# A one-core transformer block: large GpSimd operations moved to VectorE, ScalarE and TensorE

## The chip, the cores and the metric

The kernel runs as one program on one core of a Trainium2 chip. The metric is the time of one execution on the device, in microseconds (us). A core has five engines with queues of their own: TensorE (PE in the profile, its weight loads PEld), VectorE (DVE), ScalarE (ACT), GpSimd (POOL) and SyncE (SP), which here issues all transfers to 16 DMA engines.

## The reference

One block on 256 tokens of width 1024. All arithmetic is in float32.

```
mod = silu(c) @ ada_w + ada_b          # six vectors of 1024: sh1, sc1, g1, sh2, sc2, g2
h = rmsnorm(x) * (1 + sc1) + sh1
p_r, p_d, p_m = split(h @ w_in)
y_r = rwkv7_mix(p_r, ...)              # 4 heads, a recurrence over the tokens
y_d = diff_attention(p_d, ...)         # 4 heads, each the difference of two softmaxes
y_m = moba_attention(p_m, ...)         # 4 heads; one block of 256, so plain causal attention
x = x + g1 * (concat([y_r, y_d, y_m]) @ w_out)
h2 = rmsnorm(x) * (1 + sc2) + sh2
x = x + g2 * hier_moe(h2, ...)         # 32 experts, 2 of them for each token
```

## The kernel before

The program has a front and an expert stage. The front computes everything up to the sum with `g1 * mix`; the expert stage streams the weights of all 32 experts (192 MB, in 192 loads of 1 MB or their halves and quarters) through a ring of 20 buffers of 1 MB: `ringB` (10), `ringA` (2) and `ringC` (8). Most of these buffers serve the front first. The first four of `ringB` hold the RWKV part of `w_in`; the other six hold the recurrence's and the attention's tables. `ringA` holds the other pieces of `w_in` and two of the four pieces of `w_out`. `ringC` lies where the pools of the front lie. `wtile` (line 1152 on) gives buffers to the expert loads in the order ringB, ringA, ringC. A load can be issued once the tile that lay in its buffer is no longer read, and SP issues the loads one after the other.

In the front three pieces of work run interleaved. `rwkv` (the lead) is a chain of small steps. `attention` walks over 6 pairs of heads in eight steps: transposes of queries and keys (`heads_T`), logits and exponentials (`soft`), the weights (`weights`), their transposes (`probs_T`) and the products with the values. The fill work is pulled in between by `pull`, so many microseconds at a time: `proj_DM` multiplies `h` by the five pieces of `w_in` for the two attentions, in three products per step on a high part and a rest, which `split` makes (ACT copies the high part, line 313; line 314 subtracts it: on DVE for the first 16 of 40 steps, on POOL for the rest). Within `mixed`, after each unit of `proj_DM` 0.4 of a unit of the modulation follows: `columns` (sh2 and sc2, in dot products on DVE, line 364) and `gate` for g1 and g2. `gate` (line 437) multiplies 8 rows of `ada_w` by a column of silu(c) and sums them, in 16 DVE operations of 128x512 per gate, and then sums over the partitions with a matrix of ones on PE. The loads for these take turns in the two buffers of `ringF`. Loads of the front are tied to one order on SP by `load_next`.

`load_wo` (line 899) loads `w_out` in four pieces of 1 MB and multiplies each in place by g1, on POOL, in 16 operations of 128x512 (line 904). Pieces 1 and 2 lie in `ringA`, 0 and 3 in `ringF`. `proj_out` (line 907) then multiplies the mixed heads `mT` by it, in three sets: pieces 1 and 2 (diff attention), piece 0 (RWKV), piece 3 (MoBA), each as soon as its heads are done, and adds each result from PSUM to `x2` on DVE (line 925).

In `rwkv` ACT computes two sigmoids (line 535), two exponentials (lines 545 and 546) and, through `lam_of` (line 776), the exponentials of lambda. An activation function that isn't in the loaded table needs an ACT_TABLE_LOAD first. In `weights` (line 799) POOL scales one of the two exponentials (lines 805 and 808).

The order of instructions on each engine is fixed when the program is built, by a scheduler which lets a later instruction go first where an earlier one isn't ready by its own estimate; `behind` and `keep_in_program_order` tie pairs together. At run time each engine goes through its queue in that order.

Of the kernel before, what the change touches and what calls it, by code (L numbers as in the profile page):

```python
# [8 lines left out]
FT = mybir.dt.float32  # L9
# [85 lines left out]
def build(tc, ctx, a):  # L95
# [211 lines left out]
    def split(it):  # L307

        for x, (s_, k, w) in enumerate(it):
            if x == 2:  # L310
                wp[1] = fr.tile([128, 2, 2, 512], FR, name="wp1", tag="hT")
            hi, lo = (wp[x // 2 % 2][:, x % 2, q, :w.shape[-1]] for q in range(2))
            A.copy(hi, w)  # L313
            (V if x < 16 else G).tensor_sub(lo, w, hi)  # L314
            yield s_, k, hi, lo
# [104 lines left out]
    for dst_, n in ((g1b, 2), (g2b, 5)):  # L420
        G.memset(dst_, 0.0)
        load_next(dst_[0:1, :], a["ada_b"][0:1, 1024 * n:1024 * n + 1024])
# [13 lines left out]

    def gate(dst):

        for kc in range(4):
            w = take()  # L440
            for kk_ in range(2):
                for h in range(2):
                    f, k = slice(512 * h, 512 * h + 512), 2 * kc + kk_
                    V.scalar_tensor_tensor(dst[:, f], w[:, 1024 * kk_ + 512 * h:1024 * kk_ + 512 * h + 512],
                                           cs[:, k:k + 1], dst[:, f], op0=OP.mult, op1=OP.add)
            yield 0.2
        for h in range(2):
            f = slice(512 * h, 512 * h + 512)
            p = bank("bc")
            T.matmul(p, ones, dst[:, f], start=True, stop=True)  # L450
            A.copy(dst[:, f], p)
            yield 0.9
# [62 lines left out]
    def rwkv():  # L515
# [17 lines left out]
        for x, (z, b) in ((sw, (zw, "w0")), (ar, (za, "a0"))):  # L533
            for j in range(2):
                A.activation(x[:, j, :], z[:, S * j:S * j + S], AF.Sigmoid, bias=c_(b)[:, j:j + 1])
# [9 lines left out]
        A.activation(P[:, :, 1:65], c8(sw), AF.Exp, scale=lam0)  # L545
        A.activation(Pi, c8(sw), AF.Exp, scale=-lam0)
# [223 lines left out]
    def lam_of():  # L770
        lm = at.tile([128, 2, 64], FT, name="lm", tag="osq", bufs=1)
        lv = c_("lam").rearrange("p (a d) -> p a d", d=64)
        V.tensor_mul(lm, lv[:, 0::2, :], lv[:, 1::2, :])
        ls = small.tile([128, 4], FT, name="ls", bufs=1)
        V.tensor_reduce(ls[:, 0:2], lm, AX.X, OP.add)
        A.activation(ls[:, 2:4], ls[:, 0:2], AF.Exp)
        V.tensor_sub(nlam, ls[:, 3:4], ls[:, 2:3])
        V.tensor_scalar(nlam, nlam, -lam_init, None, op0=OP.add)
# [20 lines left out]
    def weights(i, e, ms, nk):  # L799
# [3 lines left out]
        if i < 4:  # L803
            V.tensor_mul(ms[:, 1:2], ms[:, 1:2], nlam)
            G.tensor_scalar(e[:, 1, :nk], e[:, 1, :nk], ms[:, 1:2], None, op0=OP.mult)
            V.scalar_tensor_tensor(w[0][:, r], e[:, 0, :nk], ms[:, 0:1], e[:, 1, :nk], op0=OP.mult, op1=OP.add)
        else:
            G.tensor_scalar(w[0][:, r], e[:, 0, :nk], ms[:, 0:1], None, op0=OP.mult)
# [90 lines left out]
    def load_wo(jj):  # L899
        w = ftile("rwo", ringF if jj in (0, 3) else ringA)  # L900
        load_next(w.rearrange("p (j n) -> p j n", j=2), wo[:, 2 * jj:2 * jj + 2, :])
        for q in range(4):
            f = slice(512 * (q % 2), 512 * (q % 2) + 512)
            G.tensor_mul(w[:, 512 * q:512 * q + 512], w[:, 512 * q:512 * q + 512], g1b[:, f])
        return w

    def proj_out():

        ws = {jj: load_wo(jj) for jj in (1, 2, 0, 3)}
        load_pk("C", const)  # L910
        for set_ in ((1, 2), (0,), (3,)):
            for j in set_:
                while ("j", 2 * j) not in done or ("j", 2 * j + 1) not in done:
                    yield WAIT
            js = [2 * j + q for j in set_ for q in range(2)]
            for t in range(NT):
                for h in range(2):
# [7 lines left out]
                    V.tensor_add(x2[:, t, f], x2[:, t, f], p)  # L925
# [5 lines left out]
    def mixed(g, h, n):  # L931
# [10 lines left out]
        yield from h  # L942
# [5 lines left out]
    g_all = chain(mixed(g_dm, chain(columns(), gate(g1b), gate(g2b)), 0.4), g_out)  # L948
# [506 lines left out]
```

## Time and profile before

| | |
|---|---|
| median of 3 runs | 717.7 us (716.8 to 719.24) |
| the profiled execution: its time | 719.76 us |
| its span, from the first to the last instruction | 718.0 us |
| mean granted TensorE clock | 0.93 |
| PE busy | 582.8 us (81%) |
| DVE busy | 284.2 us (40%) |
| ACT busy | 131.9 us (18%) |
| POOL busy | 90.0 us (13%), all of it in the first 229 us |
| HBM read | 247.66 MB, 346 GB/s over the span |

A row of a timeline gives the start in us, the duration in us, the engine, the line of the kernel, the operation, the tiles (out<-in), the shapes and the count of merged instructions; in brackets stands the idle time before it and what ended it. Line 69 and line 72 are the helper through which every matmul and transpose goes. "SPq" is SP's issuing of a transfer.

### The profile page before, as it was taken

What the parts mean: (1) busy time and instruction counts of PE and PEld (TensorE: products, weight loads), DVE (VectorE), ACT (ScalarE), POOL (GpSimd) and SP (SyncE); (2) the same over time, 40 slices, a digit from 0 to 9 for tenths busy, and PEclk for the clock granted to TensorE, in tenths of its full rate; (3) what the DMA queues carried; (4) which work ended last, traced back from release to release, by engine and by line L of the source; (5) the groups of instructions that cost most, each with busy time, mean ns of one, the idle gap of its engine ahead of it and who ended that gap; (6) DMA issues with size and microseconds to landing.
All of it is one profiled execution on the core that took longest, in us unless ns stands there. A gap on an engine that the chain in (4) does not pass through costs nothing. (4 is left out here: it accounts for less than half of the span.)

```text
span 718.0 us, 9280 instructions
## 1 busy us (share of the span) xinstructions
PE 582.8 (81%) x3548; PEld 278.9 (39%) x3548; DVE 284.2 (40%) x670; ACT 131.9 (18%) x289; POOL 90.0 (13%) x91
## 2 busy tenths in 40 slices
PE   2968979789599969799877898998686687788677
PEld 1847757576455453444222233331111124122112
DVE  5787998998665373332211122131011014002002
ACT  3374344344042041212001001010000001000000
POOL 2223148537511000000000000000000000000000
PEclk9997989989687979899999999998999899999989
DMA  8983949565036787999999999999999999999996
GB/s 359 417 330 128 423 168 366 207 215 215 1 118 234 261 325 290 418 420 419 420 422 419 421 419 421 420 419 420 421 420 419 422 406 419 421 419 420 422 383 226
DMA packets 42675, 249.36 MB, mean 347 GB/s; under 512 B 4219, under 2 KB 10243, under 8 KB 14981
## 3 DMA queue, kind: packets, MB, share of 16 engines
q1 hardware_dynamic: 42628, 248.74, 85.9%
q8 instruction: 29, 0.48, 0.3%
q14 instruction: 18, 0.14, 0.0%
HBM read 247.66 MB, written 1.06 MB: 346 GB/s over the span
## 5 line engine op out<-in xcount | busy, mean ns | idle before, releaser
L69 PE MATMUL h<-rmoe,xT 128*32 128x512 f32 (+1 forms) x1024 | 188.7, 642 | 44.5 <-DMA rmoe<-in_moe_w 44.5
L69 PE MATMUL yb<-rmoe,aTm 128*32 128x512 f32 (+2 forms) x544 | 100.4, 577 | 13.3 <-DMA rmoe<-in_moe_w 9.1
L69 PEld LDWEIGHTS h<-rmoe,xT 128*32 128x32 f32 (+1 forms) x1024 | 43.5, 119 | 172.9 <-issue 87.8
L1239 DVE TENSOR_TENSOR ac<-ac,h 128x512 f32<-128x512 f32 x9 | 6.2, 687 | 171.3 <-PE h L69 170.7
L69 PEld LDWEIGHTS yb<-rmoe,aTm 128*32 128x32 f32 (+1 forms) x544 | 27.8, 113 | 78.9 <-issue 40.7
L1274 DVE TENSOR_TENSOR yb<-yb,g2b 128x512 f32<-128x512 f32 (+1 forms) x19 | 12.6, 664 | 105.3 <-PE yb L69 105.3
L69 PE MATMUL pt<-wp,hTh 128*128 128x512 f32 (+1 forms) x160 | 53.2, 413 | 0.0
L1238 ACT ACTIVATE ac<-h 128x512 f32<-128x512 f32 x9 | 5.4, 597 | 242.5 <-PE h L69 242.5
L69 PE MATMUL cb<-yb,ST 128*128 128x512 f32 (+1 forms) x76 | 40.1, 615 | 7.0 <-DVE x L1278 6.2
L1278 DVE TENSOR_TENSOR x<-x,cb 128x512 f32<-128x512 f32 (+1 forms) x38 | 25.1, 660 | 51.6 <-PE cb L69 51.6
L69 PE MATMUL gx<-S,xn 128*128 128x128 f32 x288 | 41.4, 298 | 4.7 <-DVE S L85 2.3
L69 PEld LDWEIGHTS gx<-S,xn 128*128 128x128 f32 x288 | 37.3, 207 | 18.7 <-issue 13.4
L314 POOL TENSOR_TENSOR wp<-rwin,wp 128x512 fp32r<-128x512 f32 (+1 forms) x24 | 32.8, 1382 | 23.0 <-ACT wp L313 20.1
L1220 ACT ACTIVATE xT<-gx,sh,s2c 128x128 f32<-128x128 f32 x36 | 16.0, 456 | 99.8 <-DVE xT L1222 99.8
L69 PEld LDWEIGHTS pt<-wp,hTh 128*128 128x128 f32 x160 | 30.4, 205 | 6.8 <-ACT tq L628 0.3
L69 PE MATMUL op<-rwo,mT 128*128 128x512 f32 x64 | 32.9, 652 | 0.0
L69 PE MATMUL pt<-wp,hTl 128*128 128x512 f32 (+1 forms) x80 | 31.5, 393 | 0.0
L69 PE MATMUL pr<-hT,rwin 128*128 128x256 f32 x112 | 25.8, 390 | 2.4 <-ACT hT L372 2.4
L313 ACT CAST wp<-rwin 128x512 fp32r<-128x512 f32 (+1 forms) x40 | 22.3, 576 | 27.0 <-PE pt L69 22.7
L364 DVE CUSTOM_DVE_ANT_0 ra<-ra,mqk,pkA 128x1024 f32<-128x1024 f32 x16 | 22.3, 1395 | 8.2 <-DMA ra<-in_adaB 5.5
L364 DVE CUSTOM_DVE_ANT_0 ra<-ra,mqk,bs 128x1024 f32<-128x1024 f32 x16 | 25.4, 1587 | 0.0
L69 PEld LDWEIGHTS cb<-yb,ST 128*128 128x128 f32 x76 | 11.6, 188 | 33.8 <-DVE x L1278 21.2
(366 smaller groups left out, 633.0 us busy)
## 6 DMA issues: line engine op xcount, KB each, us to landing
rmoe<-in_moe_w SPq DMA_DIRECT2D x184, 1024.0 KB, 19.8
ra<-in_adaB SPq DMA_DIRECT2D x8, 1024.0 KB, 13.5
ra<-in_adaC SPq DMA_DIRECT2D x8, 1024.0 KB, 6.9
rwin<-in_winD SPq DMA_DIRECT2D x8, 1024.0 KB, 9.0
ra<-in_adaM SPq DMA_DIRECT2D x8, 1024.0 KB, 5.2
rwo<-in_w_out SPq DMA_DIRECT2D x4, 1024.0 KB, 7.1
rmoe<-in_moe_w SPq DMA_DIRECT2D x8, 512.0 KB, 15.4
rmoe<-in_moe_w SPq DMA_DIRECT2D x16, 256.0 KB, 5.9
```

What stands on the lines that cost most here:

```text
L69: return self._turn(self.engine.matmul(*ar, **kw))
L313: A.copy(hi, w)
L314: (V if x < 16 else G).tensor_sub(lo, w, hi)
L364: last["V"] = V.tensor_tensor_reduce(f, f, csb, 1.0, start, OP.mult, OP.add, to)
L1220: A.activation(xT[:, k, :], p[kk_ // 2][:, kk_ % 2, :], AF.Identity, bias=sh2[:, k:k + 1], scale=s2c[:, k:k + 1])
L1238: A.activation(ac, hs[0], AF.Silu)
L1239: V.tensor_mul(ac, ac, hs[1])
L1274: V.tensor_mul(yb_[:, f], py_[c], g2b[:, f])
L1278: V.tensor_add(x2[:, t, f], x2[:, t, f], p)
```

## The change

The change has six edits.

1. `split`: all 40 rests are subtracted on DVE, none on POOL.
2. `gate`: for each of the four loads of a gate PE multiplies four halves of rows (128x512) by a column of silu(c) broadcast to 32 columns, each on its own 32 columns of the array, into one bank `p`; one DVE operation adds `p` to `dst`. After the fourth, a matmul with two selecting columns (`msel`) sums over the partitions and the two rows. The starting values of g1 and g2 (`ada_b`) are loaded in two halves each.
3. The order: `mixed` gives 0.3 of a unit of the modulation to each unit of `proj_DM`, and what is left of it (the end of gate g1, gate g2) goes on at 0.3 beside `proj_out`.
4. `load_wo` doesn't multiply by g1. Pieces 0 and 3 of `w_out` take two buffers of `ringB`. The result of the first set is copied to `y` by ACT; that of the second is added to `y`, then `y` is multiplied by g1 and added to `x2`, all on DVE. Piece 3 alone is multiplied by g1 in place, by four DVE operations, ahead of the third set.
5. In `rwkv` the four sigmoids stand before the exponentials, and the exponentials of lambda after them.
6. In `weights` POOL's scaling goes to ACT for the diff heads and to DVE for the MoBA heads.

```diff
--- before.py
+++ after.py
@@ -311,7 +311,7 @@
                 wp[1] = fr.tile([128, 2, 2, 512], FR, name="wp1", tag="hT")
             hi, lo = (wp[x // 2 % 2][:, x % 2, q, :w.shape[-1]] for q in range(2))
             A.copy(hi, w)
-            (V if x < 16 else G).tensor_sub(lo, w, hi)
+            V.tensor_sub(lo, w, hi)
             yield s_, k, hi, lo
     hTh = keep.tile([128, 8, S], FR, name="hTh", tag="xn")
@@ -419,7 +419,8 @@
     g2b = keep.tile([128, D], FT, name="g2b")
     for dst_, n in ((g1b, 2), (g2b, 5)):
         G.memset(dst_, 0.0)
-        load_next(dst_[0:1, :], a["ada_b"][0:1, 1024 * n:1024 * n + 1024])
+        for h in range(2):
+            load_next(dst_[32 * h:32 * h + 1, 0:512], a["ada_b"][0:1, 1024 * n + 512 * h:1024 * n + 512 * h + 512])
     def take():
         if len(mods) < 2:
@@ -434,21 +435,25 @@
             mods.append(ftile("ra", ringF))
             load_next(mods[-1], todo_mods.pop(0))
+    msel = const.tile([128, 2], FT, name="msel")
+    V.tensor_add(msel, ident[:, 0:64:32], ident[:, 64:128:32])
+
     def gate(dst):
+
         for kc in range(4):
             w = take()
-            for kk_ in range(2):
-                for h in range(2):
-                    f, k = slice(512 * h, 512 * h + 512), 2 * kc + kk_
-                    V.scalar_tensor_tensor(dst[:, f], w[:, 1024 * kk_ + 512 * h:1024 * kk_ + 512 * h + 512],
-                                           cs[:, k:k + 1], dst[:, f], op0=OP.mult, op1=OP.add)
-            yield 0.2
-        for h in range(2):
-            f = slice(512 * h, 512 * h + 512)
-            p = bank("bc")
-            T.matmul(p, ones, dst[:, f], start=True, stop=True)
-            A.copy(dst[:, f], p)
+            p = banka("ga")
+            for g in range(4):
+                q = slice(32 * g, 32 * g + 32)
+                T.matmul(p[q, :], cs[:, 2 * kc + g // 2:2 * kc + g // 2 + 1].to_broadcast([128, 32]), w[:, 512 * g:512 * g + 512], start=True, stop=True,
+                         tile_position=(0, 32 * g))
+            V.tensor_add(dst[:, 0:512], dst[:, 0:512], p)
+            yield 1.2
+        for h in (1, 0):
+            p = banka("bc")
+            T.matmul(p, msel[:, h:h + 1].to_broadcast([128, 128]), dst[:, 0:512], start=True, stop=True)
+            A.copy(dst[:, 512 * h:512 * h + 512], p)
             yield 0.9
     def columns():
@@ -532,7 +537,7 @@
                      tile_position=(32, 0))
         for x, (z, b) in ((sw, (zw, "w0")), (ar, (za, "a0"))):
             for j in range(2):
-                A.activation(x[:, j, :], z[:, S * j:S * j + S], AF.Sigmoid, bias=c_(b)[:, j:j + 1])
+                last["A"] = A.activation(x[:, j, :], z[:, S * j:S * j + S], AF.Sigmoid, bias=c_(b)[:, j:j + 1])
         P = rp.tile([128, 8, 65], FT, name="P")
         Pi = t2("Pi", 8)
         lam0 = -math.exp(-0.5)
@@ -542,8 +547,8 @@
         for j in range(2):
             V.tensor_scalar(rkk[:, j, :], ar[:, j, :], -1.0, c_("ka")[:, j:j + 1], op0=OP.add, op1=OP.mult)
         yield 3.9
-        A.activation(P[:, :, 1:65], c8(sw), AF.Exp, scale=lam0)
-        A.activation(Pi, c8(sw), AF.Exp, scale=-lam0)
+        behind(A.activation(P[:, :, 1:65], c8(sw), AF.Exp, scale=lam0), last["A"])
+        last["A"] = A.activation(Pi, c8(sw), AF.Exp, scale=-lam0)
         PC = rp.tile([128, 8], FT, name="PC")
         V.tensor_copy(PC, P[:, :, 64])
         lam_of()
@@ -773,7 +778,7 @@
         V.tensor_mul(lm, lv[:, 0::2, :], lv[:, 1::2, :])
         ls = small.tile([128, 4], FT, name="ls", bufs=1)
         V.tensor_reduce(ls[:, 0:2], lm, AX.X, OP.add)
-        A.activation(ls[:, 2:4], ls[:, 0:2], AF.Exp)
+        behind(A.activation(ls[:, 2:4], ls[:, 0:2], AF.Exp), last["A"])
         V.tensor_sub(nlam, ls[:, 3:4], ls[:, 2:3])
         V.tensor_scalar(nlam, nlam, -lam_init, None, op0=OP.add)
@@ -802,10 +807,10 @@
         r = slice(nk - 1, None, -1)
         if i < 4:
             V.tensor_mul(ms[:, 1:2], ms[:, 1:2], nlam)
-            G.tensor_scalar(e[:, 1, :nk], e[:, 1, :nk], ms[:, 1:2], None, op0=OP.mult)
+            A.activation(e[:, 1, :nk], e[:, 1, :nk], AF.Copy, scale=ms[:, 1:2])
             V.scalar_tensor_tensor(w[0][:, r], e[:, 0, :nk], ms[:, 0:1], e[:, 1, :nk], op0=OP.mult, op1=OP.add)
         else:
-            G.tensor_scalar(w[0][:, r], e[:, 0, :nk], ms[:, 0:1], None, op0=OP.mult)
+            V.tensor_scalar(w[0][:, r], e[:, 0, :nk], ms[:, 0:1], None, op0=OP.mult)
             A.activation(w[1][:, r], e[:, 1, :nk], AF.Copy, scale=ms[:, 1:2])
         return w
@@ -897,21 +902,24 @@
     wo = a["w_out"].rearrange("(j p) n -> p j n", p=128)
     def load_wo(jj):
-        w = ftile("rwo", ringF if jj in (0, 3) else ringA)
+        w = big("rwo") if jj in (0, 3) else ftile("rwo", ringA)
         load_next(w.rearrange("p (j n) -> p j n", j=2), wo[:, 2 * jj:2 * jj + 2, :])
-        for q in range(4):
-            f = slice(512 * (q % 2), 512 * (q % 2) + 512)
-            G.tensor_mul(w[:, 512 * q:512 * q + 512], w[:, 512 * q:512 * q + 512], g1b[:, f])
         return w
     def proj_out():
+
         ws = {jj: load_wo(jj) for jj in (1, 2, 0, 3)}
         load_pk("C", const)
+        y = keep.tile([128, NT, D], FT, name="y", tag="xn")
         for set_ in ((1, 2), (0,), (3,)):
             for j in set_:
                 while ("j", 2 * j) not in done or ("j", 2 * j + 1) not in done:
                     yield WAIT
+            if set_ == (3,):
+                for q in range(4):
+                    f = slice(512 * (q % 2), 512 * (q % 2) + 512)
+                    V.tensor_mul(ws[3][:, 512 * q:512 * q + 512], ws[3][:, 512 * q:512 * q + 512], g1b[:, f])
             js = [2 * j + q for j in set_ for q in range(2)]
             for t in range(NT):
                 for h in range(2):
@@ -922,13 +930,20 @@
                         T.matmul(p, mT()[:, j, 128 * t:128 * t + 128], ws[j // 2][:, o:o + 512], start=(j == js[0]),
                                  stop=(j == js[-1]))
                         yield 0.88
-                    V.tensor_add(x2[:, t, f], x2[:, t, f], p)
+                    if set_ == (3,):
+                        V.tensor_add(x2[:, t, f], x2[:, t, f], p)
+                    elif set_ == (0,):
+                        V.tensor_add(y[:, t, f], y[:, t, f], p)
+                        V.tensor_mul(y[:, t, f], y[:, t, f], g1b[:, f])
+                        V.tensor_add(x2[:, t, f], x2[:, t, f], y[:, t, f])
+                    else:
+                        A.copy(y[:, t, f], p)
     g_dm, g_out = proj_DM(), proj_out()
     R, H = rwkv(), attention()
-    def mixed(g, h, n):
+    def mixed(g, h, n, rest=True):
         x = 0.0
         for u in g:
@@ -939,13 +954,15 @@
                 u = next(h, None)
                 if u is not None:
                     yield u
-        yield from h
+        if rest:
+            yield from h
     def chain(*gs):
         for g in gs:
             yield from g
-    g_all = chain(mixed(g_dm, chain(columns(), gate(g1b), gate(g2b)), 0.4), g_out)
+    g_mod = chain(columns(), gate(g1b), gate(g2b))
+    g_all = chain(mixed(g_dm, g_mod, 0.3, False), mixed(g_out, g_mod, 0.3))
     fill.append(g_all)
     next_mod()
     next_mod()
```

## Rows read from the trace of the kernel before

**Rows 1.** Stretches: us; busy (count) of PE, PEld, DVE, ACT, POOL; PEclk; DMA share, GB/s.

```profile
95.00:110.00 15.00, 10.67 (x56) 7.71 (x56) 13.20 (x19) 4.44 (x9) 8.72 (x7) 0.77 0.32 122
135.00:165.00 30.00, 22.73 (x253) 19.10 (x252) 27.68 (x62) 10.67 (x33) 12.81 (x13) 0.83 0.61 217
165.00:200.00 35.00, 25.56 (x265) 16.98 (x264) 24.41 (x57) 8.64 (x27) 21.47 (x18) 0.78 0.28 106
222.00:254.40 32.40, 32.40 (x112) 15.64 (x111) 10.88 (x24) 2.80 (x6) 1.52 (x2) 0.95 0.71 271
254.40:273.30 18.90, 13.27 (x105) 10.22 (x107) 16.72 (x76) 8.08 (x13) 0.00 (x0) 0.73 0.70 278
280.00:700.00 420.00, 342.86 (x1792) 113.14 (x1788) 70.48 (x149) 26.96 (x53) 0.00 (x0) 0.96 1.01 418
```

**Rows 2.** Timeline of SP's issues: loads of expert weights, the first ones.

```profile
68.54 2.12 SPq L1185 DMA_DIRECT2D rmoe<-in_moe_w  x4
...
246.03 0.80 SPq L1185 DMA_DIRECT2D rmoe<-in_moe_w  x2
254.40 2.47 SPq L1185 DMA_DIRECT2D rmoe<-in_moe_w  x5
273.29 0.33 SPq L1185 DMA_DIRECT2D rmoe<-in_moe_w  x1
```

**Rows 3.** Timeline of ACT between 42 and 57 us.

```profile
42.06 1.28 ACT L776 ACT_TABLE_LOAD   x1
...
53.46 1.28 ACT L535 ACT_TABLE_LOAD   x1
...
55.49 1.65 ACT L313 CAST wp<-rwin 128x512 fp32r<-128x512 f32 x3
```

**Rows 4.** Timeline between 93 and 103 us: DVE, POOL and PE.

```profile
93.89 1.07 DVE L171 TENSOR_SCALAR rs_t<-rs_t 128x16 f32<-128x16 f32 x1
94.89 6.20 POOL L314 TENSOR_TENSOR wp<-rwin,wp 128x512 fp32r<-128x512 f32 x5
...
99.94 1.19 DVE L175 TENSOR_TENSOR rs_t<-rs_t,rs_u 128x16 f32<-128x16 f32 x1
...
102.11 0.44 PE L72 MATMUL qk<-pkA,dqk 128*128 128x128 f32 x2 [3.71 <-DVE dqk L491]
```

**Rows 5.** Timeline between 137 and 143 us: DVE, then PE.

```profile
137.88 2.96 DVE L444 SCALAR_TENSOR_TENSOR g1b<-ra,cs,g1b 128x512 f32<-128x512 f32 x3 [1.15 <-DMA ra<-in_adaM]
140.77 0.41 DVE L629 COPY tq<-pw 128x256 f32<-128x256 f32 x1
141.24 1.97 PE L69 MATMUL pt__1124<-tq,tq 64*64 64x64 f32 x32 [4.96 <-DVE tq L629]
```

**Rows 6.** Timeline between 167 and 187 us: POOL, DVE and PE.

```profile
167.72 19.99 POOL L904 TENSOR_TENSOR rwo<-rwo,g1b 128x512 f32<-128x512 f32 x16 [3.94 <-ACT g1b L451]
178.07 1.11 DVE L185 TENSOR_SCALAR rs_v<-ssd 128x4 f32<-128x4 f32 x1
...
184.09 1.19 DVE L171 TENSOR_SCALAR rs_t<-rs_t 128x4 f32<-128x4 f32 x1
185.72 0.79 PE L69 MATMUL lg<-kT,qT 64*128 64x128 f32 x2 [6.28 <-DVE qT L763]
```

**Rows 7.** Prices: a page group, three PE timeline rows, DVE's subtractions (min/median/max ns).

```profile
L69 PE MATMUL op<-rwo,mT 128*128 128x512 f32 x64 | 32.9, 652 | 0.0
...
269.61 5.81 PE L69 MATMUL h<-rmoe,xT 128*32 128x512 f32 x52
...
125.19 0.74 PE L69 MATMUL pt<-wp,hTh 128*128 128x512 f32 x2
126.00 0.63 PE L69 MATMUL pt<-wp,hTh 128*128 128x512 f32 x2
...
L314 DVE TENSOR_TENSOR wp<-rwin,wp x16: 683/688/1722, 56.5 to 84.6; 128x512 fp32r<-128x512 f32 x16
```

**Rows 8.** The page's DMA issues: count, KB each, median us from issue to landing.

```profile
ra<-in_adaM SPq DMA_DIRECT2D x8, 1024.0 KB, 5.2
```

## The prediction

> **What bounds the kernel now.** I read the stretches first. From 280 to 700 us the DMA engines are busy throughout (share 1.01, 418 GB/s) while PE has 77 of 420 us to spare [rows 1]: in the expert stage the bytes set the time, and the change touches none of them. So the question is when the stream starts to run without a break. The issues of SP show it: four expert loads at 68.54 us, single ones as the front's tables come free, two at 246.03, five at 254.40, the next at 273.29 [rows 2]. The one at 254.40 waits for the last product with `w_out`. Call that moment L. After the five the ring of 20 is full, and the first expert products free it at 273.29. Between L and 273.3 lies the router, which the change leaves alone. A microsecond by which L comes earlier is a microsecond of the end, as long as as many loads are still to be made after L as before. Both have to be worked out: L, and that count.
>
> In the front before L I looked for time in which PE, the busiest engine there, does nothing or runs at the lower clock. In three stretches the granted clock is 0.77, 0.83 and 0.78 on the mean, so part of each is at 1.2 instead of 2.4 GHz, each time after PE had stood idle [rows 1]. At half the clock work takes twice as long, so a stretch of T us with mean clock c costs up to (1-c)T. With the idle time:
> 95 to 110: 4.3 idle, up to 3.5 from the clock; 135 to 165: 7.3 and 5.1; 165 to 200: 9.4 and 7.7.
> From 222 us to L PE is busy all the time (32.40 of 32.40) [rows 1].
>
> **Why PE stood there.** In the first stretch six DVE operations on 128x16 take 1.07 to 1.2 us each from 93.89 on, exactly while POOL makes five rests without a pause, and PE waits 3.71 us for the product behind them [rows 4]. So little data doesn't take that long: they wait for POOL. In the second, a copy that RWKV needs stands in DVE's queue behind the gate's products (three take 2.96 us, one of them after a wait for its load), and PE waits 4.96 us [rows 5]. In the third POOL multiplies `w_out` for 19.99 us on end; six DVE operations on 128x4 take 1.1 to 1.2 us each again, a query scaling stands behind them, and PE waits 6.28 us [rows 6].
>
> **What the edits take away.** (a) *Rests to DVE, no product of `w_out` on POOL.* POOL's five rests and its 16 products, beside which DVE crawled, are gone. The cover for the added DVE work: 16 rests of 128x512 at 0.69 us (median) [rows 7] and 8 of half the width, at half, make 13.8 us in the 70 us from 95 to 165; DVE loses more than that with the gates' 32 products (three in 2.96 us [rows 5]). If that cover failed, a step would have 0.69 us of DVE against six products of PE, up to 1.9 us at 0.63 for two [rows 7]; still PE. I price it at nothing.
> (b) *Gates on PE.* RWKV's copy no longer stands behind products that wait for loads on DVE.
> (c) *Sigmoids in one run.* Three table loads of 1.28 us, at 42.06, 53.46 and one between, come ahead of ACT's first high parts of `w_in` at 55.49 [rows 3]; one for the exponentials stays. At most 3.8 us, and nothing if DVE's or PE's own queue sets the start; I take 2, the middle.
> For the three stretches the lower end is the one named wait (3.7, 5.0, 6.3), the upper all idle and clock (7.8, 12.4, 17.1). I take all of the idle and a third of the clock's cost: RWKV is a chain between three engines, so some pauses stay and the clock will still fall. That gives 5.5, 9.0 and 12.0. With (c): 28.5, between 15.0 and 41.2.
>
> **What they add.** *PE in the gates.* Eight chunks of four products. The 32 calls for `w_out` leave 64 records, so a call leaves two: 64 records. The nearest row is the experts' products, of the same form, 128*32 by 128x512, four beside one another: 52 in 5.81 us, 0.112 each: 7.2 us [rows 7]. If the four didn't run beside one another, 64 records at 0.51 (32.9 us over 64) would make 32.9; in PE's pauses they would cost nothing. The row with the same form decides: 7.2. *Changes of the array's form.* After 64*64 products two `pt` take 0.74 us, after others 0.63 [rows 7]: 0.11 for each of 16 changes, 1.8, or nothing if hidden.
> The Trainium skill, TensorEngine Tiling (Array Packing), section Key Properties, says that a change of the tiling mode drains TensorE, which speaks against 32-column products strewn among full ones; it gives no price, and the row shows 0.11 us.
> *The tail.* Each result of the second set now costs DVE three operations instead of one, 2.1 us at 0.69, as much as PE's four records at 0.51; DVE is busy for 10.88 of 32.4 us there [rows 1]. Piece 3's four products, 2.8 us, are ready once g1 is, and stand in DVE's queue where the scheduler puts them. Between 0 and 5.5 us; I take 1.4, half of piece 3, as DVE is mostly idle. ACT's four copies, the scaling moved to ACT and DVE and the two small loads more replace operations of the same size or have idle engines: nothing.
> *The ring.* Pieces 0 and 3 of `w_out` take two of the four buffers from which the loads at 68.54 were made [rows 2]. Two expert loads therefore go to the back of ringB, and the second of them gets piece 3's buffer, which is read until L. The loads for ringC are behind it in SP's queue, those at 246.03 among them: nine remain at L instead of five. Four more at 2.5 us (1 MB at 418 GB/s) are 10.0; but between L and 273.3 the DMA share was 0.70 [rows 1], so 5.7 of 18.9 us were free. Net 4.3; nothing if the scheduler finds another order, 9.3 if ringA's two stand behind as well. In the front DMA has room (shares 0.32, 0.61 and 0.28 in the stretches [rows 1]), so two early loads fewer cost nothing there.
>
> **The sum.** 28.5 - 7.2 - 1.8 - 1.4 - 4.3 = 13.8 us. The profiled execution took 719.76 us, 718.0 of it span: 706.0. It lies 2.1 above the median of the runs, so 703.9 for the median.
>
> **The rivals.**
> *A. The clock stays up.* The whole of idle and clock comes back: 41.2 - 14.7 = 26.5, 691.2. For it: the pauses have the causes named, and all of them go. Against: RWKV's steps and the softmax alternate between engines.
> *B. Something else is late next.* Only the named waits go, and RWKV's chain or attention fills the rest of the pauses: 15.0 - 14.7, 717.4. For it: PE's order is fixed by a scheduler that doesn't know what will be late. Against: from 178 to 185 us nothing else was running at all.
> *C. Slower: PE waits for the gates' loads.* Before, DVE waited 1.15 us for one [rows 5] while PE could go on; now the products stand in PE's queue, and RWKV, attention and `proj_DM` stand behind them. From issue to landing a load takes 5.2 us [rows 8], and in `ringF` only one can be ahead. From 13.8 / 8 = 1.7 us for each chunk on, nothing is gained; at half of 5.2, 20.8 us are lost: 724.7. Against: PE reads a chunk in 0.9 us, so the buffer is free sooner than with four DVE products, and 0.3 of a unit for each step spreads the chunks further apart.
> *D. It doesn't do what it says.* POOL keeps the RWKV masks of 128x512 and the rests of `h`. The slowest of DVE's own 16 subtractions took 1.72 us instead of 0.69 [rows 7]; five more such waits are 5.2 us: 709.1.
> The Trainium skill's SBUF — State Buffer, section Who interferes with whom, states that DVE instructions with two SBUF inputs contend with a GpSimd operation that reads SBUF; the rests are of that kind, so by it D's waits move to them.
>
> **How the numbers follow.** The forecast (697 to 711) has 0.52, A 0.18, B 0.15, C 0.10, D 0.05. Of B, a half lies within 0.3% (2.2 us, about what a measurement of this kernel can tell from no change). Faster: 0.52 + 0.18 + 0.05 + 0.08 = 0.83; same 0.07; slower 0.10. The range from 690 to 718 takes in A and B and leaves out C and the outer ends of the costs.
>
> **What would show it.** Right: no POOL rows of `w_out` or of the last 24 rests; the six small DVE operations far below 1 us each; PE's three waits gone; L at about 236 us (254.4 - 28.5 + 7.2 + 1.8 + 1.4), and nine loads after it without a gap to the stream. Gate products at 0.11 us a record. Wrong: PE rows of the gates with idle time put down to their loads (C); a clock that is half as often and as long at 1.2 GHz (B); five loads after L (the ring priced wrongly). An L at 236 us with an end that didn't move would overturn the reading that L sets the end.

## The result, and the profile after

The changed kernel takes 698.84 us (median of four runs, 697.7 to 703.19) where the kernel before takes 717.68 beside it: a ratio of 0.9746, 95% interval 0.9701 to 0.9791. That is 18.8 us less; 13.8 were forecast. The profiled execution took 699.28 us with a span of 697.5, against 719.76 and 718.0.

The stretches of the changed kernel, columns as in [rows 1]; the last line of the fence is the whole front from 50 us to L:

```profile
95.00:110.00 15.00, 15.00 (x199) 11.70 (x198) 15.00 (x40) 7.00 (x14) 1.90 (x2) 1.00 0.89 345
135.00:165.00 30.00, 28.28 (x356) 20.07 (x354) 21.94 (x86) 15.13 (x52) 0.00 (x0) 1.00 0.80 315
165.00:200.00 35.00, 30.79 (x282) 18.37 (x283) 20.58 (x86) 12.46 (x43) 0.53 (x2) 0.90 0.61 217
231.50:250.60 19.10, 13.54 (x106) 10.14 (x108) 17.09 (x79) 8.07 (x13) 0.00 (x0) 0.73 0.96 383
280.00:690.00 410.00, 339.76 (x1719) 109.53 (x1712) 69.84 (x143) 22.39 (x46) 0.00 (x0) 0.95 1.01 417
...
50.00:231.53 181.53, 167.95 (x1446) 113.47 (x1446) 128.16 (x357) 78.25 (x191) 14.32 (x19) 0.95 0.58 216
```

And the front of the kernel before, from 50 us to its L:

```profile
50.00:254.40 204.40, 173.64 (x1381) 121.46 (x1382) 156.54 (x343) 72.51 (x178) 77.08 (x71) 0.87 0.55 209
```

What to see: in the three stretches named in the prediction PE now has 0.0, 1.7 and 4.2 us of idle time instead of 4.3, 7.3 and 9.4, and the granted clock is 1.00, 1.00 and 0.90 instead of 0.77, 0.83 and 0.78. POOL has 14.32 us of work in the front instead of 77.08. The expert stage is as it was: 417 GB/s, DMA share 1.01.

SP's issues of expert loads, as in [rows 2]:

```profile
151.11 0.92 SPq L1202 DMA_DIRECT2D rmoe<-in_moe_w  x2
...
231.53 5.51 SPq L1202 DMA_DIRECT2D rmoe<-in_moe_w  x9
...
250.57 1.75 SPq L1202 DMA_DIRECT2D rmoe<-in_moe_w  x4
```

L is at 231.53 us instead of 254.40, nine loads are made there instead of five, and the ring comes free at 250.57 instead of 273.29. Two early loads are left of four.

ACT's start, as in [rows 3]:

```profile
50.33 1.28 ACT L551 ACT_TABLE_LOAD   x1
...
53.16 1.28 ACT L540 ACT_TABLE_LOAD   x1
54.46 0.84 ACT L540 ACTIVATE tq<-za,pkA 128x256 f32<-128x256 f32 x2
55.31 1.28 ACT L550 ACT_TABLE_LOAD   x1
...
57.14 2.17 ACT L313 CAST wp<-rwin 128x512 fp32r<-128x512 f32 x4
```

Three table loads stand ahead of the casts of `w_in`, where four did from 42.06 to 53.46 us, and the casts begin at 57.14 us instead of 55.49. L551 is the second exponential (`Pi`): it runs ahead of the second pair of sigmoids (L540), so the sigmoids aren't in one run.

DVE's small operations between 93 and 200 us, grouped by form (busy us, mean ns), which answer to the ones of [rows 4] and [rows 6], and its `columns` operation:

```profile
L364 DVE CUSTOM_DVE_ANT_0 ra<-ra,mqk,bs 128x1024 f32<-128x1024 f32 x4 | 5.1, 1279 | 0.0
...
L171 DVE TENSOR_SCALAR rs_t<-rs_t 128x16 f32<-128x16 f32 x3 | 0.5, 171 | 0.0
L175 DVE TENSOR_TENSOR rs_t<-rs_t,rs_u 128x16 f32<-128x16 f32 x3 | 0.5, 165 | 0.0
...
L171 DVE TENSOR_SCALAR rs_t<-rs_t 128x4 f32<-128x4 f32 x2 | 0.3, 168 | 0.0
```

0.17 us each on the mean, where [rows 4] and [rows 6] have 1.07 to 1.19.

The third of RWKV's four blocks of 64*64 products (answers to [rows 5]); two chunks of a gate on PE, with the operations behind them (answer to the prices of [rows 7]); and the longest waits of PE between 50 us and L, in us:

```profile
129.07 1.15 PE L69 MATMUL pt__1103<-tq,tq 64*64 64x64 f32 x32 [0.30 <-DVE tq L634]
...
131.86 1.06 PE L69 MATMUL ga<-ra,cs 128*32 128x512 f32 x8
132.85 0.73 PE L69 MATMUL pt<-wp,hTh 128*128 128x512 f32 x2
...
138.84 1.06 PE L69 MATMUL ga<-ra,cs 128*32 128x512 f32 x6
139.83 0.48 PE L69 MATMUL lg<-kT,qT 64*128 64x128 f32 x2
140.25 1.04 PE L69 MATMUL ga<-ra,cs 128*32 128x512 f32 x2
141.22 1.15 PE L69 MATMUL pt__1265<-tq,tq 64*64 64x64 f32 x32
```

```profile
PE pn L69 <- ACT tq L540: 5.4, 1, 5.4
PE od L72 <- DVE dqk L855: 2.9, 1, 2.9
PE lg L69 <- DVE qT L768: 1.4, 1, 1.4
PE pt__942 L69 <- DVE tq L634: 0.9, 1, 0.9
```

The three named waits of [rows 4 to 6] (3.71, 4.96, 6.28 us) are 0.0, 0.3 and 1.4; the 0.9 before `pt__942` is that of RWKV's second block. No wait of the gates' products for their loads [rows 8] is among them. The longest one is the start's own. The second chunk was split by the scheduler: six of its records take 0.99 us to the next operation and the other two 0.97, each part as long as a whole chunk of eight.

### Where the time came from

L came 22.9 us earlier. PE's time between 50 us and L can be split into idle time, the loss from a granted clock of 1.2 GHz (half of PE's busy time in those pieces) and work at full clock. The first is read from the two front rows (204.40 - 173.64, and 181.53 - 167.95); the second is added up from the trace's steps of the granted clock.

| 50 us to L | idle | clock | work | L |
|---|---|---|---|---|
| before | 30.8 | 21.8 | 151.8 | 254.40 |
| after | 13.6 | 6.1 | 161.8 | 231.53 |
| difference | -17.2 | -15.7 | +10.0 | -22.9 |
| forecast | -23.0 | -5.4 | +10.4 | -18.1 |

(The forecast's idle is the 21.0 of the three stretches and the 2 of the sigmoids; its clock is a third of the bound of 16.3.) The span became 20.5 us shorter: 2.4 of the 22.9 were lost behind L, where 4.3 were forecast.

By place: in the three stretches 15.1 us of idle time and 11.2 of clock came back. Behind 200 us, which the prediction's sum doesn't hold, 2.7 and 5.0 more came back: before, the clock was at 1.2 GHz from 215.1 to 225.3 us, and now PE is busy at full clock from 200 us to L.

### The profile page after: what moved, and what is told of

It is laid out like the page before. It is cut to its first block, busy times and chain, and to the rows that moved or that the text cites. A ratio compares the mean times of both kernels' runs of the same rounds, so it can differ in the third digit from the quotient of the medians.

```text
span 697.5 us, 9345 instructions
## 1 busy us (share of the span) xinstructions
PE 582.4 (84%) x3612; PEld 271.3 (39%) x3612; DVE 255.7 (37%) x683; ACT 135.1 (19%) x299; POOL 28.1 (4%) x39
## 5 line engine op out<-in xcount | busy, mean ns | idle before, releaser
L69 PE MATMUL h<-rmoe,xT 128*32 128x512 f32 (+1 forms) x1024 | 191.3, 662 | 39.3 <-DMA rmoe<-in_moe_w 39.3
L69 PE MATMUL yb<-rmoe,aTm 128*32 128x512 f32 (+2 forms) x544 | 104.2, 579 | 14.2 <-DMA rmoe<-in_moe_w 9.9
L69 PE MATMUL pt<-wp,hTh 128*128 128x512 f32 (+1 forms) x160 | 51.3, 400 | 1.0 <-ACT wp L313 0.5
L69 PEld LDWEIGHTS gx<-S,xn 128*128 128x128 f32 x288 | 37.0, 207 | 15.6 <-issue 13.1
L69 PEld LDWEIGHTS pt<-wp,hTh 128*128 128x128 f32 x160 | 28.8, 195 | 9.3 <-issue 1.7
L69 PE MATMUL op<-rwo,mT 128*128 128x512 f32 x64 | 30.3, 617 | 0.0
L314 DVE TENSOR_TENSOR wp<-rwin,wp 128x512 fp32r<-128x512 f32 (+1 forms) x40 | 26.5, 683 | 3.9 <-ACT wp L313 3.8
L69 PEld LDWEIGHTS cb<-yb,ST 128*128 128x128 f32 x76 | 11.6, 188 | 36.2 <-DVE x L1295 21.2
L1239 DVE TENSOR_SCALAR xT<-gx,s2c,sh 128x128 f32<-128x128 f32 x36 | 14.4, 408 | 27.3 <-PE gx L69 27.3
L69 PEld LDWEIGHTS pr<-hT,rwin 128*128 128x128 f32 x112 | 21.0, 191 | 7.8 <-ACT hT L372 4.9
## 6 DMA issues: line engine op xcount, KB each, us to landing
ra<-in_adaB SPq DMA_DIRECT2D x8, 1024.0 KB, 13.9
```

The source lines that it names most:

```text
L69: return self._turn(self.engine.matmul(*ar, **kw))
L314: V.tensor_sub(lo, w, hi)
L1239: V.tensor_scalar(xT[:, k, :], p[kk_ // 2][:, kk_ % 2, :], s2c[:, k:k + 1], sh2[:, k:k + 1], op0=OP.mult, op1=OP.add)
```

## The experiments

The comparison of times goes by ratios to the kernel before, which stood beside each group on its chip (719.66, 718.92 and 717.59 us in the three groups). One hundredth is 7.2 us. In the whole table L and the split are those of the profiled execution, which in experiments 1, 2, 3 and 6 took 1.1 to 2.8 us more than the median.

| kernel | median | ratio (95%) | profiled | L | loads at L | idle | clock | work |
|---|---|---|---|---|---|---|---|---|
| after, again | 700.43 | 0.9754 (0.9728 to 0.9780) | 700.09 | 232.56 | 9 | 13.9 | 6.6 | 162.1 |
| 1 rests on POOL | 705.24 | 0.9803 (0.9781 to 0.9825) | 708.02 | 240.65 | 9 | 17.7 | 11.6 | 161.4 |
| 2 gates on DVE | 707.26 | 0.9824 (0.9796 to 0.9852) | 708.35 | 240.76 | 9 | 18.0 | 21.0 | 151.7 |
| 3 `w_out` on POOL | 714.30 | 0.9937 (0.9919 to 0.9955) | 715.78 | 248.19 | 9 | 22.2 | 13.1 | 163.0 |
| 4 POOL busy beside | 704.77 | 0.9801 (0.9779 to 0.9822) | 704.60 | 236.94 | 9 | 16.9 | 7.7 | 162.3 |
| 5 ring's order | 695.59 | 0.9695 (0.9668 to 0.9722) | 694.55 | 230.69 | 3 | 12.9 | 6.0 | 161.8 |
| 6 `Pi` tied | 699.38 | 0.9743 (0.9716 to 0.9770) | 701.54 | 234.08 | 9 | 12.3 | 9.7 | 162.1 |
| 7 both | 695.32 | 0.9680 (0.9656 to 0.9705) | 695.32 | 231.08 | 3 | 11.8 | 6.8 | 162.5 |
| 8 weights on POOL | 699.59 | 0.9738 (0.9706 to 0.9771) | 699.19 | 231.82 | 9 | 12.9 | 6.3 | 162.6 |
| 9 modulation at 0.4 | 701.57 | 0.9766 (0.9738 to 0.9793) | 702.24 | 234.95 | 9 | 14.7 | 7.6 | 162.7 |
| 10 before, rests alone | 709.88 | 0.9891 (0.9863 to 0.9919) | 709.31 | 244.21 | 5 | 22.3 | 17.3 | 154.6 |
| 11 before, gates alone | 707.86 | 0.9855 (0.9823 to 0.9887) | 707.39 | 243.71 | 5 | 20.0 | 12.0 | 161.7 |

The theory on trial: L sets the end; DVE's queue and its contention with POOL set L, through PE's pauses and the clock that falls behind them; each edit clears its own stretch. The rivals: the gates' move alone did it, or the start did.

**1. The rests of `w_in` on POOL again** (the changed kernel with the first edit undone).

```
-            V.tensor_sub(lo, w, hi)
+            (V if x < 16 else G).tensor_sub(lo, w, hi)
```

> The changed kernel with one part undone: the last 24 of the 40 rests are subtracted on POOL again. Theory P (POOL's large operations slow DVE's small ones, and PE then waits for DVE): the rests take some 33 us of POOL between 95 and 150 us, DVE operations beside them stretch to about 1.2 us again, and the time rises by 4 to 8 us over the changed kernel's 698.8, to 703 to 707. Rival Q (the gain came from taking the gates' products off DVE, so that the queue ahead of RWKV's copies is short): within 1.5 us of 698.8, as DVE has room for some slow operations.

Measured 705.24 us, 0.005 above the changed kernel, some 4 us, as expected; its interval overlaps that of the changed kernel's first measurement and lies just above the second's. Timeline between 94 and 103 us:

```profile
94.47 6.97 POOL L314 TENSOR_TENSOR wp<-rwin,wp 128x512 fp32r<-128x512 f32 x4 [1.87 <-ACT wp L313]
...
99.01 1.22 DVE L165 TENSOR_TENSOR rs_t<-rq 128x16 f32<-128x16 f32 x1
100.16 0.16 DVE L185 TENSOR_SCALAR rs_v<-ssq 128x16 f32<-128x16 f32 x1
100.27 1.20 DVE L166 TENSOR_TENSOR rs_t<-rs_t,rs_v 128x16 f32<-128x16 f32 x1
...
102.88 0.33 PE L72 MATMUL qk<-pkA,dqk 128*128 128x128 f32 x1 [3.48 <-DVE dqk L496]
```

The whole picture of [rows 4] is back, with the same wait (3.48 us) behind the same operation, and of the three stretches only there: the other two stay as clear as in the changed kernel. The theory of the first stretch holds. L is 9.1 us later in this execution, more than the 5.2 that the first stretch lost (3.5 idle, 1.7 of clock): between 165 and 222 us it lost 5.3 more than the changed kernel, 3.9 of it at 1.2 GHz. As it took 2.8 us more than the median, part of that second loss is its own.

**2. The gates on DVE again** (the second edit undone: 32 products on DVE, the rest as changed).

```
-                T.matmul(p[q, :], cs[...].to_broadcast([128, 32]), w[:, 512 * g:512 * g + 512], ...)
-            V.tensor_add(dst[:, 0:512], dst[:, 0:512], p)
+                    V.scalar_tensor_tensor(dst[:, f], w[...], cs[:, k:k + 1], dst[:, f], op0=OP.mult, op1=OP.add)
```

> The changed kernel with the gates as before: 16 products of 128x512 per gate on DVE, then a matrix of ones on PE. POOL stays free. Theory P: without POOL beside them the products take 0.74 us each, 24 us of DVE in all, and PE loses 7 us of work; the time rises by 0 to 4 us, to 699 to 703. Rival Q (gates on DVE were the cause): waits of 2 to 5 us of RWKV's chain for copies behind the products come back, and the time rises by 7 us or more, to 706 or later.

Measured 707.26 us: 0.007 to 0.008 above the changed kernel, some 5.5 us, and beyond the 699 to 703 of the theory: the rival, by which gates on DVE cost even without POOL, is nearer. Two stretches:

```profile
135.00:165.00 30.00, 27.31 (x326) 21.87 (x326) 25.72 (x86) 16.30 (x54) 0.00 (x0) 0.89 0.60 224
165.00:200.00 35.00, 29.64 (x221) 19.58 (x219) 26.53 (x88) 12.02 (x39) 0.53 (x2) 0.74 0.55 209
```

PE has 10.1 us less work and L still comes 9.2 later: 4.4 us more idle time and 14.9 us more at 1.2 GHz. POOL does nothing here that could crowd DVE. The products in DVE's queue are enough: PE waits 3.5 us for a copy of RWKV and 2.0 and 1.7 us for two others. Here most of the cost is clock. But the sum of the pauses alone doesn't set it: experiment 3 has more idle time (22.2 us) and loses less (13.1). In the three kernels with the gates on DVE (before, 2 and 10) the clock's loss is 0.7 to 1.2 of the idle time, in those with the gates on PE 0.45 to 0.65, and 0.8 in experiment 6. That the gates' products keep the clock up by filling PE's pauses fits these figures; it isn't shown, as no run gives PE work there that nothing needs.

**3. `w_out` multiplied on POOL again** (the gates' result applied to the weights, as before; the second gate behind the first projection).

```
+        for q in range(4):
+            f = slice(512 * (q % 2), 512 * (q % 2) + 512)
+            G.tensor_mul(w[:, 512 * q:512 * q + 512], w[:, 512 * q:512 * q + 512], g1b[:, f])
...
-                    if set_ == (3,): ...
+                    V.tensor_add(x2[:, t, f], x2[:, t, f], p)
```

> The changed kernel with the products of w_out by g1 on POOL as before (16 of 128x512, all four pieces), gate g1 therefore finished ahead of them; pieces 0 and 3 stay in ringB. Theory P: POOL works for 20 us on end, DVE's small operations beside it take 1.2 us, PE waits 5 us or more, and the first set starts later; the time rises by 8 to 13 us, to 707 to 712. Rival Q: it rises by less than 3 us. Whether contention or the wait of the products for g1 does it, the run with idle POOL work beside tells.

Measured 714.30 us: 0.019 above the changed kernel, some 13.5 us, and above the 707 to 712 expected. Timeline from 158 us:

```profile
158.29 19.85 POOL L909 TENSOR_TENSOR rwo<-rwo,g1b 128x512 f32<-128x512 f32 x16 [28.68 <-DMA rwo<-in_w_out]
...
164.76 1.19 DVE L168 TENSOR_SCALAR rd<-rs_v 128x4 int32<-128x4 int32 x1
165.99 1.19 DVE L169 TENSOR_SCALAR rd<-rd 128x4 int32<-128x4 int32 x1
...
171.09 0.69 PE L69 MATMUL pU<-R,tq 64*64 64x64 f32 x8 [5.31 <-DVE R L686]
...
176.17 0.80 PE L69 MATMUL lg<-kT,qT 64*128 64x128 f32 x4 [4.39 <-DVE qT L768]
```

POOL's block falls 9 us earlier than in [rows 6], beside a step of RWKV as well as a query scaling, so PE waits twice. The operations of 128x4 take 1.19 us again.

**4. POOL busy beside, with nothing depending on it**: the changed kernel with 16 products of `g1b`'s halves into a dead buffer.

```
+    def idle_pool():
+        for q in range(16):
+            G.tensor_mul(wp[0][:, 0, 0, :], g1b[:, 0:512], g1b[:, 512:1024])
+        yield 0.1
+    g_mod = chain(columns(), gate(g1b), idle_pool(), gate(g2b))
```

> The changed kernel with 16 products of 128x512 added on POOL that nothing reads: both halves of g1, once it is ready, into a buffer that is no longer used. No data waits for them, so only POOL's presence beside DVE is added. Theory P: 20 us of POOL, DVE's small operations in that stretch at about 1.2 us, the time rises by 4 to 10 us, to 703 to 709. Rival R (the products of w_out cost by their place in the chain g1, products, first set, not by contention): within 1.5 us of 698.8.

Measured 704.77 us, 0.005 above the changed kernel: some 3.5 us for POOL's mere presence, a little less than expected and more than the rival's 1.5. The interval of its ratio overlaps those of the changed kernel's two measurements, so the size is rough. The block, and what DVE and PE do beside it:

```profile
170.85 22.38 POOL L966 TENSOR_TENSOR wp<-g1b 128x512 fp32r<-128x512 f32 x16 [41.13 <-ACT g1b L456]
```

```profile
170.81 2.36 DVE L922 TENSOR_TENSOR rwo<-rwo,g1b 128x512 f32<-128x512 f32 x2 [0.72 <-ACT g1b L456]
...
173.09 1.48 DVE L811 SCALAR_TENSOR_TENSOR atw<-e,ms 128x256 f32<-128x256 f32 x1
...
174.49 0.55 DVE L823 COPY aT<-pa 128x384 f32<-128x384 f32 x1
...
175.09 0.94 PE L69 MATMUL po<-dv,aT 128*128 128x128 f32 x6 [3.08 <-DVE aT L823]
```

Two products and one operation that read SBUF alone take 2.36 and 1.48 us where the changed kernel has 1.29 and 0.48. The copy out of PSUM behind them keeps its 0.55, but comes late, and PE waits 3.08 us for it; the changed kernel has no such wait. DVE's small operations on 128x4 stand behind the block here, so the 1.2 us expected of them weren't put to the test. The Trainium skill, SBUF — State Buffer, section Who interferes with whom, gives DVE and GpSimd one port pair as an exclusive lock for a whole instruction. The trace agrees: the small operations of experiment 3 lose 1.02 us each (1.19 - 0.17), which is within the 1.24 us of one POOL product (19.85 / 16). A real block (experiment 3) costs more than this one because it falls on RWKV's chain; how much of the remaining 10 us is place and how much the four `w_out` pieces waiting for POOL isn't separated.

**5. The ring's order**: one load of ringB to the end of the order, so that the buffer that is read until L blocks nothing.

```
-    seq = [ringB] * NB + [ringA] * NA + [ringC] * NC
+    seq = [ringB] * (NB - 1) + [ringA] * NA + [ringC] * NC + [ringB]
```

> The changed kernel with one thing moved: in the order in which expert loads take buffers, the tenth of ringB (where piece 3 of w_out lies until the last product) comes last instead of tenth. Theory S (the loads behind that one in SP's queue are held up until the last product L, nine stand there, and the stream starts some 2.4 us late, by which the end moved less than L): fewer than nine loads remain at L, L itself stays at 231.5 within 1 us, and the time falls by 2 to 4 us. Rival T (the 2.4 us lie in the expert stage's own pace): no change within 1 us although fewer loads remain.

Measured 695.59 us against 700.43 beside it: 4.8 us faster, somewhat more than expected. SP's issues at L, then the changed kernel's and the first kernel's DMA around the moment when the ring comes free:

```profile
230.69 1.28 SPq L1202 DMA_DIRECT2D rmoe<-in_moe_w  x3
```

```profile
245.30:250.60 5.30, 5.30 (x42) 2.17 (x45) 5.16 (x22) 0.91 (x2) 0.00 (x0) 0.80 1.01 420
250.60:252.60 2.00, 2.00 (x24) 0.56 (x20) 0.45 (x5) 0.00 (x0) 0.00 (x0) 1.00 1.00 414
```

```profile
268.00:273.30 5.30, 5.30 (x44) 2.52 (x47) 5.25 (x19) 0.91 (x2) 0.00 (x0) 0.84 0.12 46
273.30:275.30 2.00, 2.00 (x24) 0.53 (x20) 0.81 (x7) 0.00 (x0) 0.00 (x0) 1.00 0.51 98
```

Three loads instead of nine are left at L. The second pair of rows is the term that the prediction missed: before the change the stream stood almost still for 5.3 us (46 GB/s) and then took 2 us to come back to speed (98 of 418 GB/s, 1.5 us lost). After it, nine loads bridge the gap.

The table shows what L does. Profiled time minus L is 467.75 us for the changed kernel, and between 467.29 and 467.66 for the other eight with nine loads at L (the repeat and experiments 1 to 4, 6, 8 and 9, L from 231.82 to 248.19). With five it is 465.36 (before), 465.10 and 463.68; with three 463.86 and 464.24. L sets the end to half a microsecond, and the four loads more cost 2.3 us against two of the three rows with five, 3.8 against the third; why the third (experiment 11) ends sooner is open.

**6. The second exponential behind the sigmoids too**: what the sigmoids' edit was meant to do.

```
+        ref = last["A"]
         last["A"] = A.activation(Pi, c8(sw), AF.Exp, scale=-lam0)
+        behind(last["A"], ref)
```

> The changed kernel with the second exponential of RWKV tied behind the last sigmoid as the first is. In the changed kernel that exponential went ahead of the second pair of sigmoids, so three table loads stand between 50 and 57 us and ACT's high parts of w_in begin at 57.1, 1.6 us later than before. Expected with the tie: one load there, high parts from about 54.6 us on, the last product with w_out 1 to 3 us earlier and the time as much shorter. Rival (DVE's or PE's own queue sets that start): high parts earlier, the time within 1 us.

Measured 699.38 us against 700.43: within 1.1 us, intervals overlapping. ACT's start:

```profile
52.20 1.28 ACT L550 ACT_TABLE_LOAD   x1
...
54.65 2.17 ACT L313 CAST wp<-rwin 128x512 fp32r<-128x512 f32 x4
```

One table load is left and the casts begin 2.5 us earlier, yet L is at 234.08 in its profiled execution, no earlier than in the changed kernel's two (231.53 and 232.56). Clock loss went from 6.1 to 9.7 us, seven of it between 165 and 222 us. What the start gains, this execution loses again later; it took 2.2 us more than the median, so part of that is its own.

**7. Both** experiments 5 and 6.

> The changed kernel with both: the tenth buffer of ringB last in the order of the expert loads, and the second exponential tied behind the sigmoids. If both theories hold and the two add, the time falls by 3 to 7 us, to 692 to 696 on a chip where the changed kernel takes 699. If neither matters, within 1 us of the changed kernel.

Measured 695.32 us, as experiment 5 alone (695.59). It is the best version here, 23.6 us below the kernel before and 5.1 below the changed one; what it has over the latter is the ring's order.

**The changed kernel once more**, beside 5 to 7:

> The changed kernel itself, unaltered, on the chip on which the next three run, so that they can be compared with it as well as with the kernel before. Every theory expects the ratio of the first measurement, 0.9746, and the last product with w_out at 231.5 us of the span.

Measured 700.43 us, ratio 0.9754, as the first time (0.9746).

**8. Attention's weights scaled on POOL again.**

```
-            A.activation(e[:, 1, :nk], e[:, 1, :nk], AF.Copy, scale=ms[:, 1:2])
+            G.tensor_scalar(e[:, 1, :nk], e[:, 1, :nk], ms[:, 1:2], None, op0=OP.mult)
```

> The changed kernel with the scaling of attention's weights back on POOL (its fifth edit undone: eight operations, four of them with the products by lambda). Theory N: these operations are few, short and have one input each, so they crowd no DVE operation, and attention's chain only swaps one engine for another: within 1.5 us of the changed kernel (698 to 702 us). Rival M: POOL takes longer for each than ACT or DVE and stands in attention's chain, which PE waits for before L: 2 to 5 us later, L at 234 us or after.

(It is the sixth edit in the list above.) Measured 699.59 us, L at 231.82: nothing, as the first theory said. POOL has 9.1 us of these operations, twelve of them in eleven pieces. So POOL's share of time isn't what costs; whether these cost nothing because they are short, few or have one input isn't separated.

**9. The modulation at 0.4.**

```
-    g_all = chain(mixed(g_dm, g_mod, 0.3, False), mixed(g_out, g_mod, 0.3))
+    g_all = chain(mixed(g_dm, g_mod, 0.4, False), mixed(g_out, g_mod, 0.3))
```

> The changed kernel with the modulation (columns and gates) advanced by 0.4 instead of 0.3 of a unit for each unit of the first projection, as before the change. Theory N: the gates' chunks come earlier but are the same work, and no wait for their loads appears (each load of 1 MB lands some 5 us after its issue, chunks would still be 6 us or more apart): within 1.5 us (698 to 702). Rival C, what is left of it: chunks closer together outrun the single load that can be ahead, and PE shows waits put down to the DMA of ra, 2 us or more in sum: 702 to 708.

Measured 701.57 us, ratio 0.9766; the interval holds the changed kernel's. No wait for `ra` shows although chunks stand at 156.81, 160.78 and 164.66 us, 3.9 apart: rival C falls once more. L is 3.4 us later in its profile; there PE waits 2.7 us for rests on DVE. Whether 0.4 is slower at all is left open.

**10 and 11. One edit alone, in the kernel before.** First the rests, then the gates.

```
-            (V if x < 16 else G).tensor_sub(lo, w, hi)
+            V.tensor_sub(lo, w, hi)
```

> The kernel before with the first edit alone: all rests on DVE, everything else as it was (gates on DVE, products of w_out on POOL). Undone alone this edit cost 4 to 6 us. Theory A (parts add up): it brings as much alone, 712 to 715 us, with the small operations after 93 us below 0.5 us each and PE's wait there gone. Rival O (they overlap): DVE has the gates' products and 14 us of rests more, so the stretch from 95 to 110 us gains 3 to 6 us and the one from 135 to 165 loses part of it again: 715 to 719.

> The kernel before with the second edit alone: both gates as 32-column products on PE, rests and products of w_out on POOL as they were. Undone alone this edit cost 7 us. Theory A (parts add up): it brings 5 to 8 us alone, 710 to 713 us. Rival O (they overlap): it costs PE 8 us of its own and takes away only the queue on DVE between 135 and 165 us; POOL's 20 us of w_out still crowd DVE after 165: 714 to 719, with PE's wait for the query scaling still 4 us or more.

Measured 709.88 us (7.7 us faster) and 707.86 us (9.7 faster): both faster than either theory had it. The stretches, the rests alone first:

```profile
95.00:110.00 15.00, 14.89 (x115) 10.98 (x115) 14.97 (x33) 7.67 (x16) 0.07 (x1) 1.00 0.64 250
135.00:165.00 30.00, 24.30 (x226) 17.77 (x225) 27.73 (x64) 9.21 (x29) 10.48 (x9) 0.89 0.71 262
```

```profile
95.00:110.00 15.00, 10.65 (x57) 7.81 (x57) 12.85 (x19) 4.09 (x8) 8.25 (x7) 0.77 0.35 134
135.00:165.00 30.00, 29.70 (x359) 21.62 (x357) 17.10 (x52) 12.77 (x36) 8.31 (x11) 1.00 0.34 124
```

Each edit clears its own stretch and leaves the other's much as it was in [rows 1]: the rests the one from 95 us, the gates the one from 135. But the parts don't add up. Alone the two bring 17.4 us, nearly as much as the whole; undone from the whole they cost some 4 and 5.5. And the whole without the edit of `w_out` (experiment 3) gains only 5.4, less than either alone by 2.3 and 4.3. Most of that gap are its nine loads at L against five: profiled time minus L is 2.5 and 3.9 us longer than theirs. That it gains no more than they do, though it has both edits, points at POOL's remaining block: in the gates-alone kernel the block is cut in three and PE loses 8.8 idle and 5.9 of clock between 155 and 222 us; where it runs on end PE loses 13.5 and 10.5 (experiment 3) and 12.0 and 11.2 (rests alone). That the cut makes this difference is read from three kernels, not tried by itself. `w_out`'s edit alone wasn't run.

## Why the prediction was right, and where it was not

The sign, the bound and most of the places were right. **L sets the end**: shown by the constant distance between L and the end in nine executions with nine loads. **Contention**: right; experiments 1 and 3 bring the slow operations back with their waits, 4 without any dependence. **Gates on PE**: with 0.112 a record and two form changes a chunk 9.0 us were forecast. Measured to the next operation it is 9.0 too, but put together otherwise: seven whole chunks of 0.99 to 1.08 us, not 1.12, and 1.96 for the one that was split. The Trainium skill, TensorEngine Tiling (Array Packing), section Key Properties, lets a change of mode drain TensorE; the trace leaves it at most 0.1 us a chunk (0.99 against eight records at 0.112), so it doesn't decide. All of PE's added work was 10.0 us; the 10.4 forecast hold 1.4 for DVE's tail, which cost no pause (PE is busy from 200 us to L), so the other 1.0 has no place in the forecast. **Nine loads at L**: right.

Where it failed, by its own terms:

- *A third of the clock's cost.* The largest error: 5.4 forecast, 15.7 came back. Of the 10.3 more, 5.0 lie behind 200 us, for which its sum has nothing; nearly all of the rest is that in the stretches 11.2 came back and not a third of the bound. The reason given, that RWKV's alternation would keep some pauses and with them the low clock, is wrong in its second half: 13.6 us of pauses did stay, but of the front behind 50 us only the pieces from 52.9 to 63.1 and from 192.8 to 199.6 us ran at 1.2 GHz. Experiment 2 shows the other side, where 4.4 us of pauses more, with the gates' work gone from PE, stand beside 14.9 us more of clock loss. Rival A had the mechanism, and the time lies between it (691.2) and the forecast.
- *All of the idle time of the stretches.* 15.1 us came back in them instead of 21.0: some pauses stand there still, the largest, a new one, of 2.9 us before `od` (193.9 us). With 2.1 us from elsewhere it is 17.2.
- *The sigmoids in one run, 2 us.* Zero. Only `P` was tied, and the scheduler put `Pi` between the sigmoid pairs; the prediction read the edit as if order in the code were order on ACT. By experiment 6 the term itself was worth nothing that can be told from zero: the casts begin 2.5 us earlier, L doesn't, and the median falls by 1.1 us with overlapping intervals (by 0.3 from 5 to 7).
- *The ring, 4.3 us.* 2.3 by two rows with five loads. The free 5.7 us between L and the ring's release were counted, the 1.5 us that the stopped stream needed to get going again were not; that leaves 2.8, so 0.5 stay open. What the ring's order costs in all, nine loads against three, is 3.5 us by the rows and 4.8 by the medians.
- *Rival C* fell: no wait for the gates' loads in the changed kernel, and none with closer chunks (9). *B* fell: 32.9 us of idle time and clock came back, not the 15.0 of the named waits. *D* fell by the time (709.1 against 698.8), and in experiment 8 still more small operations on POOL cost nothing.

In sum the clock gave 10.3 us more than forecast and the idle time (the start's 2 in it) 5.8 less, the work cost 0.4 less and the ring 1.9 less: 6.8 us, as the spans show within 0.1 (20.5 against 13.8). The medians show 5.0 of it (18.8 against 13.8). That the total came so close is partly luck: the clock's error was twice as large, and the idle time's stood against it.

## What to carry to other kernels

Look for the moment that sets the end and measure each variant by it: here the end is L plus a constant, and the constant changes only with what is queued behind L. Price a pause of TensorE with the clock that falls behind it, since that can be worth more than the pause, and expect that the parts of a change that clears pauses may not add up. When a step depends on an order, tie every instruction of it: one that is left free may be scheduled into the run.

## What the runs showed that I had not expected

The `columns` operation on DVE (128x1024, one of each pair) took longer before the change, too:

```profile
L364 DVE CUSTOM_DVE_ANT_0 ra<-ra,mqk,bs 128x1024 f32<-128x1024 f32 x4 | 7.2, 1789 | 0.0
```

1789 ns against 1279 after. The mean hides two kinds: the two at 104 and 107 us, while POOL makes no rests, took 1.28 us each; the two at 112 and 118 us, beside its rests, 2.28 and 2.31. So large operations of DVE lose about as much time as the small ones, only by a smaller factor. And POOL loses in its turn: four rests took 6.97 us in experiment 1, 1.74 each, against 1.24 for a product of the same size in experiment 3. In the kernel before, the stopped stream of loads ran for 2 us at 98 GB/s before it was back at speed; with nine loads at L there is no such stop, so four loads more in the queue cost less than their bytes.
